# Block C's gates and output products by feature tile and spread over its steps, x in single k tiles, the last output bank in two halves

## The chip, the core and the metric

The kernel runs on one core of one Trainium2 chip. The core has a matrix engine (TensorE, PE in the profile), a vector engine (VectorE, DVE), an activation engine (ScalarE, ACT), GpSimd (POOL) and SyncE (SP), which here issues every DMA. The metric is the device time of one launch in microseconds (us), the median of some runs. The matrix engine multiplies a stationary block of 128x128, loaded into it by a weight load, with a moving operand of up to 512 columns, and adds up in PSUM, whose banks hold 512 float32 in each partition. Every engine works through its own instructions in the order in which the program has them.

## The reference

Three blocks over 256 tokens of width 1024: a retention layer (A), a latent attention layer (B), and a hybrid layer (C) of a recurrent branch, a sparse attention branch and a feed-forward network. A and B end in a layer norm. The change is mostly in C:

```
h = rms_norm(x, norm1_w);  u = h @ w_in          # split: rnn_x, rnn_gate, q, k, v, iq, ik, iw, g
xc = causal_depthwise_conv(rnn_x, conv_w, conv_b)
y_rnn = rg_lru(xc, ...) * gelu(rnn_gate)         # gates r, i; linear recurrence over the tokens
y_attn = dsa_attention(q, k, v, iq, ik, iw)      # top-64 keys by index score, softmax, 16 heads
gates = sigmoid(g + gate_b)                      # two branches of 1024 features
merged = gates[0] * (y_rnn @ w_o_rnn) + gates[1] * (y_attn @ w_o_attn)
x = x + merged @ w_out
x = x + square(relu(rms_norm(x, norm2_w) @ w_ff_in)) @ w_ff_out
```

## The kernel before

**Products in three parts.** Float32 operands are split into a rounded high part (`split`, L241 to L243: a cast on ACT, L242) and the rest as a low part (a subtraction on DVE, L243). A product is then three matmuls (`mm3`, L293 to L296: high by high, high by low, low by high, recorded as L294, L295 and L296).

**Weights in pieces.** `plan` lists all weights in the order of their use, as pieces of up to 1024 columns. `take` hands out the next piece and calls `fetch` for those up to seven further on (`AHEAD`): a DMA into a raw tile (4 buffers, or a `t2` tile for the small ones of the opening), then the split into a `whl` tile (8 buffers, two of which C's recurrence takes over). So each piece of 1024 costs ACT and DVE one instruction each, whatever product it goes into.

**Two forms of product.** `tpart` and `tgemm` have tokens on the partitions: the activation of 128 tokens is stationary and a piece of 512 features moves. `ftile` has features on the partitions: 128 features of the weights are stationary and 256 tokens move; one unit is 8 k tiles x 3 = 24 matmuls into one accumulator. Accumulators come from the pool `acc` of four PSUM banks; transposes use two banks (`tr`), attention two (`att`).

**The opening.** x and the first two weights come by k tiles, in groups of 1, 1, 2, 2 and 2 (`OPENING`); `values_and_gates` multiplies each group as it comes.

**The end of B.** `proj` runs B's output product; `norm1` calls `normal` (layer norm: sums on DVE, squares on ACT), then C's own norm and its transposes, for each half of the tokens.

**Block C.** Index projections, keys and values, and queries are `tgemm`s; the queries are copied by ACT (L993) and transposed at once. DVE picks 64 keys per token by eight rounds of `max` and `match_replace` (L983, L984) and writes the mask `sel` (L985). Then the table `STEPS` orders the rest by hand: `x` convolution of one feature tile (`conv`: a unit, then three DVE steps, L1085), `g` gelu gate (`gelu`: a unit, its second product on DVE is L1113), `z` recurrence gates (`gates`: two small float32 products, L1094, read by ACT at L1096 and L1097), `a` attention (`attend`: scores and softmax of one pair of heads, and the values of the pair before, all at high priority), `r` recurrence, `G` a gate product of 512 features (bias row added by DVE, L1151, then tanh), `O` an output product of 512 features (`gated`: times the gate, both branches added, transposed for the last product, L1152 to L1173). The four G and four O stand at the table's end. Within what the table and the priorities leave open, a scheduler puts each engine's instructions in order when the kernel is built.

**The end.** The feed-forward's output product adds up in four banks (two halves of the tokens by two halves of the features). After the last group each bank is scaled, added to x (L1262) and stored (L1263).

## Time and profile before

| what | value |
|---|---|
| time, 3 runs | median 893.03 us (891.98 to 893.21) |
| the profiled execution | 892.43 us, of which the span of its instructions 890.6 us |
| PE busy | 875.2 us (98%), 5471 matmuls |
| weight loads (PEld) busy | 784.4 us (88%) |
| DVE busy, ACT busy | 620.8 us (70%), 504.3 us (57%) |
| DMA | 157.16 MB, mean 176 GB/s |
| granted clock of PE | 1.00 throughout (2.4 GHz) |

Matmuls overlap each other in the records: one lasts longer than the distance to the next one's start. What a stream of them costs is read from the starts. Idle time of PE is listed with the engine and line that ended it; idle time of DVE and ACT costs nothing by itself.

### The profile page before, as it was taken

Reading aid. Unit: us, or ns where it says so; the run is one execution under the profiler, and the core shown is the slowest. Engines: PE = TensorE matmul, PEld = TensorE weight load, DVE = VectorE, ACT = ScalarE, POOL = GpSimd, SP = SyncE. Lnnn points to the kernel's source line nnn. Section 1 sums busy time; section 2 is a strip of 40 time slices with the busy share of each in tenths; the row PEclk is TensorE's granted clock in tenths of the full one; section 3 lists DMA queues with packets and bytes.
Section 4 is the critical chain, followed back from the end, with each engine's and each line's share of the span. In section 5 each row is a group of like instructions: output and inputs, shape, how many; then the busy total and the mean of one; then the engine's idle time right before and its main releaser. Section 6 shows DMA issues by size and latency. Waiting matters only on the chain.

```text
span 890.6 us, 14371 instructions
## 1 busy us (share of the span) xinstructions
PE 875.2 (98%) x5471; PEld 784.4 (88%) x5471; DVE 620.8 (70%) x1155; ACT 504.3 (57%) x860; POOL 40.8 (5%) x45
## 2 busy tenths in 40 slices
PE   8999999999999999999999999999999999999998
PEld 6988898889999999998878798987788889999997
DVE  5886776758766777676677799778766756555551
ACT  5644445435766676665458678987643455444440
POOL 0000000100100000002111020000000100000000
PEclk9999999999999999999999999999999999999999
DMA  8955455744654453546537634243765556556531
GB/s 295 310 190 171 160 170 185 274 134 159 231 166 153 144 165 132 177 143 247 185 116 223 216 100 148 84 143 119 248 203 179 187 164 212 190 188 190 190 119 48
DMA packets 47446, 157.16 MB, mean 176 GB/s; under 512 B 5392, under 2 KB 6160, under 8 KB 47248
## 3 DMA queue, kind: packets, MB, share of 16 engines
q1 hardware_dynamic: 47376, 156.23, 52.6%
q8 instruction: 43, 0.70, 0.3%
q14 instruction: 27, 0.22, 0.1%
HBM read 155.16 MB, written 1.05 MB: 175 GB/s over the span
## 4 chain that ended last, share of the span: by engine, by line
PE 86%; DVE 7%; ACT 2%; issue 2%; DMA 1%; SPq 0%; POOL 0%; ACTq 0%; DVEq 0%
PE acc L294 23%; PE acc L296 23%; PE acc L295 23%; PE att L294 4%; PE att L296 4%; PE att L295 4%; PE tr L215 2%; DVE whl L243 2%; DMA raw<-wpk 1%; PE att L1050 1%; DVE t L1085 1%; DVE s L984 1%; DVE sm L983 0%; DVE buf L1123 0%; PE att L404 0%
## 5 line engine op out<-in xcount | busy, mean ns | idle before, releaser
L243 DVE TENSOR_TENSOR whl<-raw,whl 128x1024 fp32r<-128x1024 f32 (+2 forms) x285 | 335.8, 1187 | 152.0 <-ACT whl L242 149.6
L242 ACT CAST whl<-raw 128x1024 fp32r<-128x1024 f32 (+2 forms) x285 | 288.3, 1021 | 218.1 <-PE acc L296 121.4
L294 PE MATMUL acc<-whl,s 128*128 128x512 f32 (+3 forms) x592 | 219.8, 377 | 2.5 <-DVE t L1151 1.2
L296 PE MATMUL acc<-whl,s 128*128 128x512 f32 (+3 forms) x592 | 221.6, 375 | 0.0
L295 PE MATMUL acc<-whl,s 128*128 128x512 f32 (+3 forms) x592 | 220.7, 373 | 0.5 <-DVE whl L243 0.5
L294 PE MATMUL acc<-s,whl 128*128 128x256 f32 x600 | 170.5, 284 | 2.7 <-ACT t L1097 1.3
L296 PE MATMUL acc<-s,whl 128*128 128x256 f32 x600 | 169.1, 282 | 0.0
L295 PE MATMUL acc<-s,whl 128*128 128x256 f32 x600 | 168.9, 282 | 0.0
L294 PEld LDWEIGHTS acc<-whl,s 128*128 128x128 f32 x592 | 111.3, 188 | 22.4 <-ACT whl L242 2.4
L296 PEld LDWEIGHTS acc<-whl,s 128*128 128x128 f32 x592 | 111.4, 188 | 18.9
L295 PEld LDWEIGHTS acc<-whl,s 128*128 128x128 f32 x592 | 111.4, 188 | 18.8 <-DVE whl L243 1.0
L294 PEld LDWEIGHTS acc<-s,whl 128*128 128x128 f32 x600 | 113.5, 189 | 4.3 <-ACT t L1097 1.7
L295 PEld LDWEIGHTS acc<-s,whl 128*128 128x128 f32 x600 | 113.5, 189 | 0.4
L296 PEld LDWEIGHTS acc<-s,whl 128*128 128x128 f32 x600 | 113.5, 189 | 0.1
L296 PE MATMUL att<-s,whl 128*128 128x256 f32 x224 | 62.9, 281 | 0.0
L294 PE MATMUL att<-s,whl 128*128 128x256 f32 x224 | 62.9, 281 | 0.0
L295 PE MATMUL att<-s,whl 128*128 128x256 f32 x224 | 62.9, 281 | 0.0
L294 PE MATMUL acc<-whl,hh 128*128 128x512 f32 x128 | 49.9, 389 | 0.0
L295 PE MATMUL acc<-whl,hh 128*128 128x512 f32 x128 | 49.8, 389 | 0.0
L296 PE MATMUL acc<-whl,hh 128*128 128x512 f32 x128 | 49.4, 390 | 0.0
L296 PEld LDWEIGHTS att<-s,whl 128*128 128x128 f32 x224 | 42.9, 191 | 0.1
L295 PEld LDWEIGHTS att<-s,whl 128*128 128x128 f32 x224 | 42.1, 188 | 0.6
(252 smaller groups left out, 1078.8 us busy)
## 6 DMA issues: line engine op xcount, KB each, us to landing
raw<-wpk SPq DMA_DIRECT2D x249, 512.0 KB, 4.1
raw<-wpk SPq DMA_DIRECT2D x32, 384.0 KB, 3.2
row<-rows SPq DMA_DIRECT2D x18, 256.0 KB, 6.5
t<-wpk SPq DMA_DIRECT2D x7, 256.0 KB, 5.6
raw<-wpk SPq DMA_DIRECT2D x4, 328.0 KB, 3.4
xs<-xtok SPq DMA_DIRECT2D x1, 1024.0 KB, 6.8
wb<-wab SPq DMA_DIRECT2D x4, 256.0 KB, 5.8
out<-t SPq DMA_DIRECT2D x4, 256.0 KB, 2.0
```

Source lines behind the costliest of these rows:

```text
L215: flips.append(nc.tensor.transpose(dst, src, ident))
L242: (copy or A.copy)(h, src)
L243: V.tensor_sub(l, src, h.bitcast(F32))
L294: return [mm(ps, lhsT=ah, rhs=bh, start=st, stop=False), mm(ps, lhsT=ah, rhs=bl, start=False, stop=False), mm(ps, lhsT=al, rhs=bh, start=F ...
L295: mm(ps, lhsT=ah, rhs=bl, start=False, stop=False),
L296: mm(ps, lhsT=al, rhs=bh, start=False, stop=sp)]
L984: V.match_replace(out=score[:, c], in_to_replace=s[:, 0:8], in_values=score[:, c], imm_value=GONE)
L1050: mm(o[:, 0:256], lhsT=vC[:, 0, g, j], rhs=pts[j][:, 0:256], start=j == 0, stop=False)
L1085: V.scalar_tensor_tensor(xc[:, d:], px[:, :256 - d], cw[:, m, j:j + 1], xc[:, d:], op0=ALU.mult, op1=ALU.add)
```

## The change

- x, and the first two weights with it, come in eight single k tiles.
- The gate and output products become `ftile` units: 16 `G` steps (8 for each branch) and 16 `O` steps of 128 features. The gate's bias is now a column and goes into the tanh on ACT; the four bias rows and their DVE additions go. A gate lies in 256 columns of a tile kept until its `O` step. `gated` leaves the result with features on the partitions, which is how the next product wants it: the 16 transposes behind it go, and its split reads the tile instead of PSUM.
- `STEPS` spreads x, G, z, g and a evenly; G10 to G17 run around the recurrence, the O steps stand at the end.
- The transposes of the queries are put off by two `take`s.
- In `attend`, matmuls and transposes lose their high priority; softmax, the copies behind the transposes and the split keep it.
- In `normal` the low parts of the `ckv` pieces fetched so far are ordered behind the mean.
- In the last group the fourth bank is closed one group earlier, added to x as `rest`, and the last products go in two halves of 256 columns into `tr` banks, each stored by itself.

```
-OPENING = ((0, 1), (1, 1), (2, 2), (4, 2), (6, 2))
+OPENING = tuple((k, 1) for k in range(8))
-STEPS = ("w0 w1 b x0 x1 x2 x3 g0 z0 g1 x4 a z1 g2 x5 a z2 g3 x6 a z3 g4 x7 a z4 g5 a z5 g6 a z6 g7 a "
-         "G00 z7 r a G01 a G10 G11 O00 O01 O10 O11").split()
+STEPS = ("w0 w1 b x0 G00 G01 x1 z0 g0 a x2 G02 z1 g1 a x3 G03 z2 g2 a x4 G04 z3 g3 a x5 G05 z4 g4 a x6 G06 z5 g5 "
+         "a x7 G07 z6 g6 a G10 z7 g7 a G11 r G12 G13 a G14 G15 G16 G17 "
+         "O00 O01 O02 O03 O04 O05 O06 O07 O10 O11 O12 O13 O14 O15 O16 O17").split()
...
+        low = split(hl[:, :w], hl[:, 1024:1024 + w], raw[:, :w])
+        if name == "ckv":
+            kvsplits.append(low)
...
-        V.tensor_scalar(nm, s[:, 0:1], s[:, 1:2], -1.0 / 1024.0, op0=ALU.add, op1=ALU.mult)
+        mean = V.tensor_scalar(nm, s[:, 0:1], s[:, 1:2], -1.0 / 1024.0, op0=ALU.add, op1=ALU.mult)
+        for low in kvsplits:
+            order(low, mean)
...
+            defer(DEFER_Q, lambda c=c, t=t, q=q: turn_queries(c, t, q))
...
+        urgent(softmax, p, scs, pbs, s, mx, nb)
...
-            A.copy(pt[:, :384], pp[:, :384])
+            urgent(A.copy, pt[:, :384], pp[:, :384])
...
-        split(ya[0][:, p], ya[1][:, p], o[:, 0:256])
+        urgent(split, ya[0][:, p], ya[1][:, p], o[:, 0:256])
...
-        with tc.high_priority():
-            nxt = scores(p + 1) if p < 7 else None
-            if p >= 0:
-                values(p, pend["pbs"])
+        nxt = scores(p + 1) if p < 7 else None
+        if p >= 0:
+            values(p, pend["pbs"])
...
-    def gate_gemm(br, n):
-        gb = row(f"gb{br}{n}")[0]
-        gps = tgemm(f"cg{br}", 4, hT)
-        for t in range(2):
-            w = gts[br, n, t] = t2()
-            V.tensor_add(w, gps[t], gb)
-            A.activation(out=w, in_=w, func=AF.Tanh, scale=0.5)
+    def gate(br, m):
+        ps = acc()[:, 0:256]
+        ftile(ps, take(f"cg{br}"), 0, hT)
+        if (br, m // 2) not in gts:
+            gts[br, m // 2] = rowp.tile([P, 512], F32, tag="row", name="gate") if (br, m) == (0, 0) else t2()
+        w = gts[br, m // 2][:, (m % 2) * 256:(m % 2) * 256 + 256]
+        A.activation(out=w, in_=ps, func=AF.Tanh, scale=0.5, bias=hbg[:, 8 * br + m:8 * br + m + 1])
...
+    def gated(br, m):
+        ps = acc()[:, 0:256]
+        ftile(ps, take(("cor", "coa")[br]), 0, (yr, ya)[br])
+        w, w0 = (gts[i, m // 2][:, (m % 2) * 256:(m % 2) * 256 + 256] for i in (br, 0))
         V.scalar_tensor_tensor(w, w, 1.0, ps, op0=ALU.add, op1=ALU.mult)
...
-        V.tensor_add(w, w, gts[0, n, t])
-        transposed(w, 4 * n, 4, mT, t, scale=0.5)
+        V.tensor_add(w, w, w0)
+        h, l = mT[0][:, m], mT[1][:, m]
+        A.activation(out=h, in_=w, func=AF.Copy, scale=0.5)
+        V.scalar_tensor_tensor(l, w, 0.5, h.bitcast(F32), op0=ALU.mult, op1=ALU.subtract)
...
+                corner = t == n == 1
+                if corner and g == NFG - 1:
+                    continue
...
+                if g == NFG - 1:
+                    store(t, c, fps[t][n], xs[:, t, c])
...
+        rest = t2()
+        V.scalar_tensor_tensor(rest, fps[1][1], r3[:, 1:2], xs[:, 1, 512:1024], op0=ALU.mult, op1=ALU.add)
+        for i in range(2):
+            c = slice(512 + i * 256, 768 + i * 256)
+            ps = tr()[:, 0:256]
+            for m in ms:
+                mm3(ps, hh[:, 0, m, tk], hh[:, 1, m, tk], pcs[m].h[:, 0, c], pcs[m].l[:, 0, c],
+                    m == 0, m == ms[-1])
+            store(1, c, ps, rest[:, i * 256:i * 256 + 256])
```

Three places show how the engines' orders move. The first is VectorE at the layer norm of the second half of the tokens at B's end: L553 makes the sums, L555 the mean (L555 and L557 after), L848 (L854) scales by it, and `whl` are splits of weight pieces. Before:

```order
L553 SCALAR_TENSOR_TENSOR t2_4876,sm_4878<-xs_1503,acc_4670 128x512
L243 TENSOR_TENSOR whl_4765<-raw_4763,whl_4765 128x1024
L553 SCALAR_TENSOR_TENSOR t2_4877,sm_4878<-xs_1503,acc_4671 128x512
L243 TENSOR_TENSOR whl_4926<-raw_4924,whl_4926 128x1024
L555 TENSOR_SCALAR sm_4878<-sm_4878 128x1
L848 SCALAR_TENSOR_TENSOR t2_4885<-t2_4876,sm_4878,row_4529 128x512
L848 SCALAR_TENSOR_TENSOR t2_4886<-t2_4877,sm_4878,row_4532 128x512
```

The same place after:

```order
L555 SCALAR_TENSOR_TENSOR t2_4919,sm_4921<-xs_1545,acc_4713 128x512
L555 SCALAR_TENSOR_TENSOR t2_4920,sm_4921<-xs_1545,acc_4714 128x512
L243 TENSOR_TENSOR whl_4969<-raw_4967,whl_4969 128x1024
L557 TENSOR_SCALAR sm_4921<-sm_4921 128x1
L243 TENSOR_TENSOR whl_4808<-raw_4806,whl_4808 128x1024
L854 SCALAR_TENSOR_TENSOR t2_4928<-t2_4919,sm_4921,row_4572 128x512
L854 SCALAR_TENSOR_TENSOR t2_4929<-t2_4920,sm_4921,row_4575 128x512
```

One of two splits ahead of the mean now stands directly behind it, still ahead of the two scalings.

The second place is VectorE in C's steps, at the last rounds of the choice of keys: MAX and MATCH_REPLACE are that choice, `qks` the stacked queries, L1085 the convolution (L1098 after), L1111 and L1113 the two products of a gelu gate (L1124 and L1126 after), `whl` splits of weights. Before, down to the mask:

```order
L243 TENSOR_TENSOR whl_5693<-raw_5691,whl_5693 128x1024
L1111 SCALAR_TENSOR_TENSOR t2_5766<-t2_5766,acc_5736 128x256
L983 MAX sm_5308<-s2_4922 128x8
L984 MATCH_REPLACE s2_4922<-sm_5290,s2_4922 128x128
L243 TENSOR_TENSOR whl_5739<-raw_5737,whl_5739 128x1024
L1085 SCALAR_TENSOR_TENSOR t2_5801<-acc_5771,pcol_1504,t2_5801 128x255
L984 MATCH_REPLACE s2_4922<-sm_5308,s2_4922 128x256
L1113 SCALAR_TENSOR_TENSOR buf_5547<-t2_5766,acc_5736 128x256
L985 TENSOR_SCALAR tab_4551<-s2_4922 128x128
L1085 SCALAR_TENSOR_TENSOR t2_5801<-acc_5771,pcol_1504,t2_5801 128x254
L985 TENSOR_SCALAR tab_4551<-s2_4922 128x256
```

The same place after:

```order
L243 TENSOR_TENSOR whl_5694<-raw_5692,whl_5694 128x1024
L1098 SCALAR_TENSOR_TENSOR t2_5721<-acc_5691,pcol_1546,t2_5721 128x253
L1124 SCALAR_TENSOR_TENSOR t2_5767<-t2_5767,acc_5737 128x256
L395 TENSOR_TENSOR qks_4960<-tr_5620,qks_4960 64x512
L990 MATCH_REPLACE s2_4965<-sm_5351,s2_4965 128x256
L991 TENSOR_SCALAR tab_4594<-s2_4965 128x128
L243 TENSOR_TENSOR whl_5740<-raw_5738,whl_5740 128x1024
L1126 SCALAR_TENSOR_TENSOR buf_5575<-t2_5767,acc_5737 128x256
L991 TENSOR_SCALAR tab_4594<-s2_4965 128x256
```

By the mask VectorE stood in the fifth convolution and the second gelu gate (`acc_5771`, `acc_5736`); it now stands in the second convolution and the first gelu gate (`acc_5691`, `acc_5737`).

The third place is VectorE at the program's end, which is new (L1278 is the last step of a bank, L1267 is `rest`):

```order
L1278 SCALAR_TENSOR_TENSOR t2_9334<-acc_7917,tiny_83,xs_1545 128x512
L1278 SCALAR_TENSOR_TENSOR t2_9343<-acc_7918,tiny_83,xs_1545 128x512
L1278 SCALAR_TENSOR_TENSOR t2_9352<-acc_7919,tiny_83,xs_1545 128x512
L1267 SCALAR_TENSOR_TENSOR t2_9355<-acc_7920,tiny_83,xs_1545 128x512
L1278 SCALAR_TENSOR_TENSOR t2_9364<-tr_9357,tiny_83,t2_9355 128x256
L1278 SCALAR_TENSOR_TENSOR t2_9374<-tr_9367,tiny_83,t2_9355 128x256
```

`rest`, whose bank is closed first of all, stands behind the step of the third bank.

## Rows read from the trace of the kernel before

**Rows 1.** The page, busy time of each engine (share of the span) and instructions:
```profile
PE 875.2 (98%) x5471; PEld 784.4 (88%) x5471; DVE 620.8 (70%) x1155; ACT 504.3 (57%) x860; POOL 40.8 (5%) x45
```

**Rows 2.** Waits of PE: line, releaser, us in total, times, longest:
```profile
PE att L1050 <- ACT t L1046: 1.5, 1, 1.5
PE acc L294 <- ACT t L1097: 1.3, 1, 1.3
PE acc L294 <- DVE buf L1113: 1.2, 1, 1.2
...
PE acc L294 <- DVE t L1151: 1.2, 1, 1.2
PE tr L215 <- ACT t L993: 1.1, 1, 1.1
PE tr L215 <- DVE t L819: 1.0, 1, 1.0
...
PE tr L215 <- ACT t L1046: 0.4, 1, 0.4
```

**Rows 3.** Timeline of PE (start, us, instruction) in three steady stretches; weight loads:
```profile
402.10 0.28 PE L295 MATMUL acc<-s,whl 128*128 128x256 f32 x1
...
403.98 0.28 PE L296 MATMUL acc<-s,whl 128*128 128x256 f32 x1
659.82 0.39 PE L294 MATMUL acc<-whl,s 128*128 128x512 f32 x1
...
663.94 0.39 PE L294 MATMUL acc<-whl,s 128*128 128x512 f32 x1
677.67 1.03 PE L215 MATMUL tr<-ident,t 128*128 128x128 f32 x8
L294 PEld LDWEIGHTS acc<-s,whl 128*128 128x128 f32 x600 | 113.5, 189 | 4.3 <-ACT t L1097 1.7
```

**Rows 4.** Busy time in stretches: PE, PEld, DVE, ACT, POOL, clock, DMA:
```profile
500.00:560.00 60.00, 55.70 (x429) 52.37 (x428) 55.17 (x171) 44.02 (x89) 6.56 (x4) 1.00 0.40 132
560.00:600.00 40.00, 40.00 (x256) 36.26 (x255) 30.06 (x92) 34.53 (x87) 0.00 (x0) 1.00 0.37 124
```

**Rows 5.** Timeline of PE in the opening, with idle time and releaser:
```profile
9.32 0.72 PE L294 MATMUL acc<-whl,s 128*128 128x512 f32 x2 [0.56 <-ACT whl L242]
12.97 0.50 PE L295 MATMUL acc<-whl,s 128*128 128x512 f32 x1 [0.54 <-DVE whl L243]
```

**Rows 6.** Timeline at B's last layer norm:
```profile
457.08 1.22 DVE L243 TENSOR_TENSOR whl<-raw,whl 128x1024 fp32r<-128x1024 f32 x1
458.21 0.21 DVE L555 TENSOR_SCALAR sm<-sm 128x1 f32<-128x1 f32 x1
458.46 1.42 DVE L848 SCALAR_TENSOR_TENSOR t<-t,sm,row 128x512 f32<-128x512 f32 x2
460.16 0.21 DVE L562 TENSOR_SCALAR sm<-sm 128x1 f32<-128x1 f32 x1 [0.28 <-ACT t L558]
```

**Rows 7.** Timeline at the start of C's steps:
```profile
510.77 0.65 PE L215 MATMUL tr<-ident,t 128*128 128x128 f32 x4 [1.06 <-ACT t L993]
510.96 0.61 DVE L983 MAX8 sm<-s 128x8 f32<-128x128 f32 x2
527.47 1.02 PE L1094 MATMUL acc<-t,wb 128*128 128x256 f32 x4
528.40 0.86 DVE L1085 SCALAR_TENSOR_TENSOR t<-acc,pcol,t 128x255 f32<-128x255 f32 x2
541.15 0.28 DVE L985 TENSOR_SCALAR tab<-s 128x256 f32<-128x256 f32 x1
```

**Rows 8.** The end: last matmul, last step, the stores; a step of 256 columns:
```profile
886.48 0.39 PE L296 MATMUL acc<-whl,hh 128*128 128x512 f32 x1
886.90 0.75 DVE L1262 SCALAR_TENSOR_TENSOR t<-acc,tiny,xs 128x512 f32<-128x512 f32 x1 [0.15 <-PE acc L296]
out<-t SPq DMA_DIRECT2D x4, 256.0 KB, 2.0
L1113 DVE SCALAR_TENSOR_TENSOR buf<-t,acc 128x256 f32<-128x256 f32 x8 | 3.3, 412 | 0.0
```

More of the change, by code (lines that the diff above doesn't have):

```diff
@@ L117, in plan @@
         elif op in "GO":
-            br, n = arg
-            for j in range(4):
-                if op == "G":
-                    o = og + br * 1024 + n * 512
-                    add(f"cg{br}", "c_in", 2 * j, 2, ar(o, o + 512))
-                else:
-                    add(("cor", "coa")[br], ("o_rnn", "o_att")[br], 2 * j, 2, ar(n * 512, n * 512 + 512))
+            br, m = arg
+            if op == "G":
+                o = og + br * 1024 + m * 128
+                add(f"cg{br}", "c_in", 0, 8, ar(o, o + 128))
+            else:
+                add(("cor", "coa")[br], ("o_rnn", "o_att")[br], 0, 8, ar(m * 128, m * 128 + 128))
     for k in range(8):
@@ L239, in body, with split @@
     wide_home = {}
-    def split(h, l, src, copy=None):
-        (copy or A.copy)(h, src)
-        V.tensor_sub(l, src, h.bitcast(F32))
+    def split(h, l, src):
+        A.copy(h, src)
+        return V.tensor_sub(l, src, h.bitcast(F32))
     def fetch():
@@ L988, in body, with turn_queries @@
     rq = tiny[:, 40:72].rearrange("p (t h) -> p t h", t=2)
+    def turn_queries(c, t, q):
+        p2 = tr()
+        for i in range(4):
+            transpose(p2[:, i * 128:i * 128 + 128], q[:, i * 128:i * 128 + 128])
+        p2 = p2.rearrange("p (k n) -> p k n", k=4)
+        if t == 0:
+            A.copy(q0[:, 4 * c:4 * c + 4], p2)
+        else:
+            stacked(p2, qs[c], 4)
     for c in range(2):
@@ L998, in body @@
             rsqrt(rq[:, t, c * 8:c * 8 + 8], s[:, 0:8], 8, 1.0, 64e-6)
-            p2 = tr()
-            for i in range(4):
-                transpose(p2[:, i * 128:i * 128 + 128], q[:, i * 128:i * 128 + 128])
-            p2 = p2.rearrange("p (k n) -> p k n", k=4)
-            if t == 0:
-                A.copy(q0[:, 4 * c:4 * c + 4], p2)
-            else:
-                stacked(p2, qs[c], 4)
+            defer(DEFER_Q, lambda c=c, t=t, q=q: turn_queries(c, t, q))
     yr = []
@@ L1022, in scores, with softmax @@
             half_product(scs[j][:, 128:384], parts(qs[blk], j, p % 4), kh[j][:, blk], kl[:, j, blk])
+        urgent(softmax, p, scs, pbs, s, mx, nb)
+        return pbs
+    def softmax(p, scs, pbs, s, mx, nb):
         for j in range(2):
@@ L1191, in body @@
         elif op == "G":
-            gate_gemm(*arg)
+            gate(*arg)
         else:
-            out_gemm(*arg)
+            gated(*arg)
     w2 = row("norm2")
@@ L1245, in ff_out, with store @@
                 c = slice(n * 512, n * 512 + 512)
+                corner = t == n == 1
+                if corner and g == NFG - 1:
+                    continue
                 for m in ms:
                     mm3(fps[t][n], hh[:, 0, m, tk], hh[:, 1, m, tk], pcs[m].h[:, 0, c], pcs[m].l[:, 0, c],
-                        g == 0 and m == 0, g == NFG - 1 and m == ms[-1])
+                        g == 0 and m == 0, g == NFG - 1 - corner and m == ms[-1])
+                if g == NFG - 1:
+                    store(t, c, fps[t][n], xs[:, t, c])
+        if g < NFG - 1:
+            return
+        rest = t2()
[7 more added lines that the diff above has]
+            store(1, c, ps, rest[:, i * 256:i * 256 + 256])
+    def store(t, c, ps, x):
+        o = t2()[:, :c.stop - c.start]
+        V.scalar_tensor_tensor(o, ps, r3[:, t:t + 1], x, op0=ALU.mult, op1=ALU.add)
+        dma(out[t * 128:t * 128 + 128, c], o)
     ff_in(0)
@@ L1257, in body @@
         ff_out(g)
-    for t in range(2):
-        for n in range(2):
-            c = slice(n * 512, n * 512 + 512)
-            o = t2()
-            V.scalar_tensor_tensor(o, fps[t][n], r3[:, t:t + 1], xs[:, t, c], op0=ALU.mult, op1=ALU.add)
-            dma(out[t * 128:t * 128 + 128, c], o)
 def constants():
@@ L1316, in pack @@
             "idxn": g["idx_k_norm_w_2"][0], "qkn": np.concatenate([g["q_norm_w_2"][0], g["k_norm_w_2"][0]])}
-    for br in range(2):
-        for n in range(2):
-            rowv[f"gb{br}{n}"] = g["gate_b_2"][0, br, n * 512:n * 512 + 512]
     flatrow = np.concatenate([rowv[n] for n, _ in ROWS])
```

22 lines of the change are left out of this document (6 added, 16 removed).

## The prediction

> **What bounds the kernel now.** I read the busy times first [rows 1]. PE is busy for 875.2 of the 890.6 us of the span (98%); DVE and ACT stand at 70% and 57%. So a change can only take PE's work away, or the 15 us in which PE stands still. The second view is the list of PE's waits [rows 2]: besides many of a few tenths there are seven single ones of 0.4 to 1.5 us, and all seven lie where this change moves something. The third is the spacing of the matmuls [rows 3], since their own lengths overlap: 256 columns take (403.98 - 402.10) / 16 = 0.118 us from start to start, 512 columns (663.94 - 659.82) / 18 = 0.229 us, a transpose about (1.03 - 0.28) / 7 = 0.11 us. The records last 0.28 and 0.39 us, 0.16 us more than the spacing. So a wait that lets the pipe run empty costs its listed time and 0.16 us on top. The fourth is a table of two stretches of C's steps [rows 4]: in 500 to 560 DVE is busy for 55.17 of 60 us, in 560 to 600 for 30.06 of 40. In the first it is the late engine, in the second it is not.
>
> **PE's own work.** Gates and output products in units of 24 matmuls of 256 columns instead of 12 of 512, and the end's 6 of 512 as 12 of 256: by the order of both kernels +780 matmuls of 256, -390 of 512 and -16 transposes. 780 x 0.118 - 390 x 0.229 - 16 x 0.11 = 92.0 - 89.3 - 1.8, about **+1.0 us**. There are 374 more weight loads, 189 ns each [rows 3]. I cost them at nothing, since the stretch at 402 us has one load of 189 ns for each matmul of 256 columns and yet starts one every 0.118 us: loads run beside matmuls and beside one another. Without that cover the price is rival C.
>
> The Trainium skill ("TensorE: Matmul & The Clock Gate", Part 3, "What overlaps and what doesn't") speaks against the change: it lets a weight load overlap matmuls in flight only where the row groups differ, and all loads here use all rows. By that rule the sum would be the one of rival C. The trace disagrees: loads of 189 ns fit between starts 118 ns apart [rows 3].
>
> **The opening.** x comes in eight pieces instead of five. PE waits twice [rows 5]: 0.56 us for the second k tile's split on ACT, 0.54 us for that of the third on DVE. The first six transfers are the same in both kernels, so the first wait stays. The third k tile is now half as large a transfer and half as long a split: that wait goes, 0.54 + 0.16 = **-0.7 us** (bounds 0 and -1.4).
>
> **B's last norm.** PE waits 1.04 us, shown as 1.0 [rows 2], for C's norm (L819), at the end of a chain on DVE and ACT: sums, a split of a weight piece (458.21 - 457.08 = 1.13 us), mean, two scalings (1.42), and the step at 460.16 that waits for the squares on ACT [rows 6]. The order takes one of two splits from ahead of the mean. It puts it directly behind, still ahead of the scalings. So the mean and with it the squares come 1.13 us earlier, but the scalings do not; the step at 460.16 now follows DVE's own queue, and of its wait of 0.28 us with the step from engine to engine about 0.35 is gained: **-0.35 us** (bounds 0 and -1.2, the whole wait and the drained pipe).
>
> **Queries.** Each query is transposed at once, and the last waits 1.06 us for the copy [rows 7]. Put off by two takes, the transposes stand behind a whole unit of 24 matmuls (24 x 0.118 = 2.8 us), which covers the copy: 1.06 + 0.16 = **-1.2 us** (bounds -0.7 and -1.3).
>
> **The steps' waits.** The other five of [rows 2] end on L1046 (twice, the copy of the transposed probabilities), L1097, L1113 and L1151. L1151 and its bias rows no longer exist; in the other places units G or x now stand between producer and user. What goes is 1.5 + 1.3 + 1.2 + 1.2 + 0.4 = 5.6, with 5 x 0.16 for the pipe **-6.4 us**. What is late next has to be put against it.
>
> **New: gelu 1.** There are four accumulator banks; the fifth user behind gelu 0 (x2, G02, the two of z1 in between) is gelu 1, and it takes gelu 0's bank. So it waits until DVE has done gelu 0's second product (L1113, L1126 after). DVE is without a gap from the first MAX at 510.96 to the mask's end at 541.15 [rows 7]. By the two orders the stretch that ends with that product of gelu 0 lacks, of the work that before did up to the mask, one split (1.13 [rows 6]), eight convolution steps (0.86 / 2 = 0.43 each [rows 7]) and two gelu products (0.41 each [rows 8]): 5.4 by durations, which overlap a little, so I take 5.0. That product is then done at about 541.15 - 5.0 = 536.2. PE, 1.06 us earlier at the first query's wait, has from 510.77 - 1.06 = 509.7 on seven units (168 x 0.118 = 19.8), 16 transposes (1.8), two z of 4 small products (1.02 - 0.16 = 0.86 each [rows 7]) and one pair's scores (8 matmuls of up to 256 columns, 0.9): it stands at gelu 1 at 533.9. The difference is 2.3, and 1.9 with the 5.4: **+2.0 us** for one wait. Bounds: 0, if DVE's split runs ahead as it may, and 4, if it is the full unit late.
>
> **New: the recurrence and the last pairs.** The last pair's transposes need some 18.5 to 19 us of DVE's and ACT's work behind gelu 7, and PE's units up to them make about 19 us. That is a tie. The same two instructions (L1046 to L1050) cost 1.5 before [rows 2]; my value is **+0.5 us** (bounds 0 and 1.5).
>
> **The tail.** Before, the last matmul starts at 886.48, a step of 0.75 us follows, and a store of 256 KB lands after 2.0 us [rows 8]. After, the last step has 256 columns (0.41 by L1113 [rows 8]), but it stands in DVE's queue behind the third bank's step and `rest`, 0.75 each. The third bank closes 12 x 0.118 = 1.4 us before the last matmul; 0.75 + 0.75 + 2 x 0.41 = 2.3 us from there is 0.9 behind the last matmul, just where the step before ended (0.15 + 0.75). So DVE brings nothing. The store is half as large. If its time went by its bytes it would gain 1.0 of the 2.0 us, if it is all fixed nothing; no row shows a store of 128 KB, and I take a tenth, nearer to fixed, since the other half's transfer goes out just ahead of it: **-0.2 us** (bounds +0.2, where DVE's steps come out longer, and -1.0).
>
> **The sum.** -0.7 - 0.35 - 1.2 - 6.4 + 1.0 + 2.0 + 0.5 - 0.2 = -5.35 us. The profiled execution took 892.43 us (its span 890.6), so it would be 887.1; the median is 893.03, and with the same difference it becomes **887.7 us** (0.994). A measurement of this kernel tells about 0.2% (1.8 us) from no change: faster is below 891.2, slower above 894.8.
>
> **Rivals.** (A) *No new wait.* DVE and ACT run ahead, since the copies and softmax keep their priority and the bias additions are gone. For it: 30.06 of 40 us busy in the second stretch [rows 4]. Against: DVE has no gap up to the mask [rows 7]. Without the 2.0 and 0.5: -7.85, that is 885.2 us. Chance 0.18.
> (B) *The waits come back elsewhere.* DVE's rounds of keys have as much work as before (55.17 of 60 us [rows 4]) and PE reaches them earlier, so banks come free late not once but at several gelu and convolution units, until the new waits are as large as the old: 6.4 in place of 2.5. Then -1.45, 891.6 us, no difference that can be told. Against: the order leaves convolutions for later that DVE did before the mask. Chance 0.12.
> (C) *Slower: the added weight loads show.* Where a unit's loads aren't hidden, 374 x 189 ns = 70.7 us come on top: 958 us. It decides from 7.1 / 374 = 19 ns for each added load on (no difference from 10 ns: 3.6 / 374). Against it stands the spacing at 402.10 [rows 3], in exactly that form of unit; for it only that the gates' stationary blocks come from pieces of another layout, and PEld is busy for 88% of the span already [rows 1]. Chance 0.05.
> (D) *Parts that do nothing.* The opening's wait only moves, the norm's chain ends with its scalings as before, the store costs the same: +1.25 on the forecast, 889.0 us. Chance 0.05.
>
> **How the numbers follow.** The forecast has 0.60, with a range of its own of 886.0 to 889.5 (the wait at gelu 1 between 0.5 and 3.5 and the tie between 0 and 1.5). The range of 8 in 10 is 884.0 to 891.6: from A with the opening at its better bound to B. C and half of B lie outside, and a little of the ends of A. Faster by over 0.2%: 0.60 + 0.18 + 0.05 and a little of B, 0.85; within: most of B, 0.10; slower: C, 0.05.
>
> **What would show it.** In the profile of the changed kernel PE's busy time rises by about 1 us, and 256 columns stay at 0.118 us from start to start in the G and O units; over 0.13 means C. The list of PE's waits has no L1151, no L993, and the one for L1126 at gelu 1 of 1 to 3 us near 534 to 536; several of over 1 us on DVE mean B, none means A. The wait at 12.97 is gone and the one at 9.32 still there. L819's wait is about 0.7. The last store lands as late behind the last matmul as before, or 0.3 us earlier. Wrong would be the prediction above all if DVE's order at the mask ran otherwise in time than I laid it out from the durations before.

## The result and the profile after

The changed kernel takes 886.95 us (median of six runs, 886.35 to 887.40) against 892.05 us before (six runs). The ratio is 0.994 with a 95% interval of 0.9928 to 0.9953, that is -5.1 us, between -4.2 and -6.4. The forecast was 887.7 us, -5.35. Of the profiled executions 892.43 us became 887.0; the spans are 890.6 and 885.2, both at a granted clock of 1.00 (2.4 GHz).

The sum came out, and several of its terms did not. The page of the changed kernel, busy time and instructions, to be held against [rows 1]:

```profile
PE 873.5 (99%) x5845; PEld 801.4 (91%) x5845; DVE 619.5 (70%) x1171; ACT 508.0 (57%) x881; POOL 39.1 (4%) x45
```

PE's waits in the changed kernel (line, releaser, us in total, times, longest), to be held against [rows 2]:

```profile
PE acc L296 <- DVE t2r L243: 2.3, 1, 2.3
PE acc L296 <- ACT tr L1012: 1.5, 1, 1.5
...
PE acc L296 <- DVE buf L1126: 0.8, 1, 0.8
PE tr L214 <- DVE t L825: 0.6, 1, 0.6
```

All five waits of the steps are gone, the copies of the probabilities (L1046) among them. The norm's wait (L825, L819 before) is down from 1.04 to 0.6. The queries' wait is still there, at another place and longer (L1012: 1.5 instead of L993: 1.1). The wait at gelu 1 (L1126) has come, with 0.8 instead of 2.0 us. And at the top stands one that the forecast does not have: 2.3 us for a split near 29 us. Timeline of ACT, DVE and PE there:

```profile
23.62 1.06 ACT L242 CAST whl<-raw 128x1024 fp32r<-128x1024 f32 x1 [0.18 <-DMA raw<-wpk]
26.88 1.05 ACT L242 CAST whl<-raw 128x1024 fp32r<-128x1024 f32 x1 [2.20 <-PE acc L298]
27.84 0.58 ACT L242 CAST t2r<-acc 128x512 fp32r<-128x512 f32 x1
...
27.96 1.22 DVE L243 TENSOR_TENSOR whl<-raw,whl 128x1024 fp32r<-128x1024 f32 x1 [2.02 <-ACT whl L242]
...
29.11 0.68 DVE L243 TENSOR_TENSOR t2r<-acc,t2r 128x512 fp32r<-128x512 f32 x1
...
29.84 0.39 PE L296 MATMUL acc<-s,whl 128*128 128x256 f32 x1 [2.29 <-DVE t2r L243]
```

Read it from the bottom. PE needs a bank of `acc`; the bank is free when DVE has split the values out of it (29.11); DVE needs ACT's copy (27.84), and ACT's copy stands in ACT's queue behind the copy of a large weight piece, for which ACT had stood idle for 2.2 us.

Where the time went can be read from three landmarks. Timeline of PE, the last product of the index scores and the last matmul, in the kernel before (the second is the first of [rows 8]) and in the changed one:

```profile
509.44 0.28 PE L404 MATMUL att<-ix 128*128 128x256 f32 x1
```

```profile
509.83 0.28 PE L406 MATMUL att<-ix 128*128 128x256 f32 x1
...
881.00 0.28 PE L298 MATMUL tr<-whl,hh 128*128 128x256 f32 x1
```

Up to the index scores the changed kernel loses 0.4 us (the opening loses 0.8, the norm gives 0.4 back). The 0.8 is one profile against one: the first matmul behind the opening starts anywhere from 28.1 to 29.4 us in the profiles of kernels with the old opening, and from 28.6 to 29.9 with the new one. From the last product of the index scores to the last matmul the changed kernel takes 371.17 us instead of 886.48 - 509.44 = 377.04: -5.9. From the last matmul's start to the end of the span it takes 4.2 us instead of 4.1.

### The profile page after: what moved, and what is told of

It reads as the page before. It is cut to its first block, busy times and chain, and to the rows that moved or that the text cites. A ratio compares the mean times of both kernels' runs of the same rounds, so it can differ in the third digit from the quotient of the medians.

```text
span 885.2 us, 15181 instructions
## 1 busy us (share of the span) xinstructions
PE 873.5 (99%) x5845; PEld 801.4 (91%) x5845; DVE 619.5 (70%) x1171; ACT 508.0 (57%) x881; POOL 39.1 (4%) x45
## 3 DMA queue, kind: packets, MB, share of 16 engines
HBM read 154.12 MB, written 1.05 MB: 175 GB/s over the span
## 4 chain that ended last, share of the span: by engine, by line
PE 94%; DVE 3%; ACT 2%; issue 1%; POOL 0%; DVEq 0%; ACTq 0%
PE acc L296 25%; PE acc L298 25%; PE acc L297 25%; PE att L296 4%; PE att L297 4%; PE att L298 4%; PE tr L214 3%; DVE whl L243 1%; PE att L1063 1%; PE acc L1107 1%; PE att L405 0%; PE att L406 0%; PE acc L452 0%; PE att L758 0%; PE att L730 0%
## 5 line engine op out<-in xcount | busy, mean ns | idle before, releaser
L243 DVE TENSOR_TENSOR whl<-raw,whl 128x1024 fp32r<-128x1024 f32 (+1 forms) x279 | 328.0, 1186 | 138.1 <-ACT whl L242 136.8
L242 ACT CAST whl<-raw 128x1024 fp32r<-128x1024 f32 (+1 forms) x279 | 282.1, 1020 | 215.3 <-PE acc L298 108.7
L296 PE MATMUL acc<-s,whl 128*128 128x256 f32 x856 | 243.6, 285 | 4.6 <-DVE t2r L243 2.3
L298 PE MATMUL acc<-s,whl 128*128 128x256 f32 x856 | 241.6, 282 | 0.0
L297 PE MATMUL acc<-s,whl 128*128 128x256 f32 x856 | 241.4, 282 | 0.0
L298 PE MATMUL acc<-whl,s 128*128 128x512 f32 (+3 forms) x464 | 171.0, 369 | 0.0
L297 PE MATMUL acc<-whl,s 128*128 128x512 f32 (+3 forms) x464 | 170.5, 368 | 0.0
L296 PE MATMUL acc<-whl,s 128*128 128x512 f32 (+3 forms) x464 | 169.7, 372 | 0.5 <-ACT s L242 0.5
L296 PEld LDWEIGHTS acc<-s,whl 128*128 128x128 f32 x856 | 161.7, 189 | 6.3 <-DVE t2r L243 2.7
L297 PEld LDWEIGHTS acc<-s,whl 128*128 128x128 f32 x856 | 162.3, 190 | 0.5
L298 PEld LDWEIGHTS acc<-s,whl 128*128 128x128 f32 x856 | 161.8, 189 | 0.2
L296 PEld LDWEIGHTS acc<-whl,s 128*128 128x128 f32 x464 | 87.5, 189 | 14.8 <-ACT s L242 1.3
L298 PEld LDWEIGHTS acc<-whl,s 128*128 128x128 f32 x464 | 87.4, 188 | 13.7
L297 PEld LDWEIGHTS acc<-whl,s 128*128 128x128 f32 x464 | 87.3, 189 | 12.7
L296 PE MATMUL acc<-whl,hh 128*128 128x512 f32 x126 | 49.1, 390 | 0.0
L297 PE MATMUL acc<-whl,hh 128*128 128x512 f32 x126 | 49.0, 389 | 0.0
L298 PE MATMUL acc<-whl,hh 128*128 128x512 f32 x126 | 48.8, 390 | 0.0
```

The source lines that it names most:

```text
L242: A.copy(h, src)
L243: return V.tensor_sub(l, src, h.bitcast(F32))
L296: return [mm(ps, lhsT=ah, rhs=bh, start=st, stop=False), mm(ps, lhsT=ah, rhs=bl, start=False, stop=False), mm(ps, lhsT=al, rhs=bh, start=F ...
L297: mm(ps, lhsT=ah, rhs=bl, start=False, stop=False),
L298: mm(ps, lhsT=al, rhs=bh, start=False, stop=sp)]
```

## The experiments

Ratios are to the kernel before, run beside each; the changed kernel's is 0.994. The span is that of the one profiled execution.

| kernel | ratio | 95% interval | span |
|---|---|---|---|
| e1_open | 1.0002 | 0.9992 to 1.0011 | 893.2 |
| e3_defer | 1.0004 | 0.9994 to 1.0013 | 891.3 |
| e12_prio | 0.9956 | 0.994 to 0.9973 | 886.8 |
| e4_steps | 0.9976 | 0.9964 to 0.9987 | 886.7 |
| e11_attend | 0.9941 | 0.9926 to 0.9956 | 885.4 |
| e2_last2 | 0.9928 | 0.9913 to 0.9943 | 885.3 |
| e8_valsplit | 0.9907 | 0.9891 to 0.9922 | 884.2 |
| e5_query | 0.9976 | 0.9964 to 0.9987 | 890.9 |
| e7_late | 0.9942 | 0.9927 to 0.9957 | 887.1 |
| e6_rest | 0.9931 | 0.9916 to 0.9946 | 883.7 |
| e9_best | 0.9892 | 0.9878 to 0.9907 | 882.1 |
| e10_gelu | 0.9889 | 0.9875 to 0.9904 | 881.8 |

The granted clock of PE is not 1.00 in all of these runs. In the profiles of e1_open, e7_late, e8_valsplit and e5_query it stands at 0.5 (1.2 GHz) for one stretch or two; the last section has the rows. Spans are therefore compared by stages below, and a difference of under 1 us between two kernels of the table is not read from times.

### The opening

**e1_open** is the kernel before with one line of the change:

```diff
-OPENING = ((0, 1), (1, 1), (2, 2), (4, 2), (6, 2))
+OPENING = tuple((k, 1) for k in range(8))
```

> The kernel before, with x and the first two weights in eight single k tiles and nothing else changed. Theory 1 (the opening costs): the waits of 0.56 and 0.54 us go, and a new one of about 2.3 us stands at the first unit of 256 columns near 28 us, as in the profile of the changed kernel; -0.56 - 0.54 - 2 x 0.16 + 2.3 + 0.16 is +1.0 us, a time ratio of about 1.001. Theory 2 (the prediction): one wait goes and nothing comes, -0.7 us; the new wait then belongs to some other part of the change.

Measured: +0.2 us (-0.7 to +1.0). Its list of waits has neither of the two of [rows 5] and a new one on top:

```profile
PE acc L294 <- DVE t2r L243: 2.0, 1, 2.0
```

So the 2.3 us belong to the opening, and they take back what the two old waits gave. The time alone decides nothing: the forecast's -0.7 lies at one edge of the interval and the +1.0 of theory 1 at the other. The new wait in the list speaks for theory 1. Of the two old waits the first is no firm gain: it is missing also from the lists of e3_defer and e12_prio, which have the old opening. The span of 893.2 holds, besides the wait, a stretch at a granted clock of 0.5 right behind it (29.7 to 33.1 us).

**e8_valsplit** changes only the order of two kinds of copies on ACT, in the changed kernel (piece 28 is the fifth large weight piece):

```diff
+        casts.append(A.copy(h, src))
...
+        piececast[i] = casts[-1]
...
                     for t in range(2):
                         split(*d["v"][t], vps[t])
+                        if h == 0:
+                            order(piececast[28], casts[-1])
```

> The changed kernel; only ACT's order is changed at 27 us: the rounding copies of the two value banks (first half of the split of the values) stand ahead of the copy of the fifth large weight piece, whose transfer lands at 26.85. Theory 1 (ACT waits in its queue for a late transfer, and the split that frees the bank stands behind it): the wait of 2.3 us goes, to 0 to 0.3; -2.2 to -2.4 us, a profiled span of about 883. Theory 2 (the banks are closed too late, three matmuls apart, for any split to be in time): most of the 2.3 us stays.

Measured: 0.9907, about 2.9 us less than the changed kernel's 0.994 (expected 2.2 to 2.4; the intervals of the two ratios reach 1.1 and 1.4 us to either side). The wait is not in its list any more, and the first matmul behind the opening starts at 27.4 us instead of 29.8. Theory 1 stands: the banks close early enough, and what cost the time was an instruction that waits for a transfer, ahead of one that had all it needed. The transfer is late because of the pieces: eight groups of half-size weight pieces go through `t2` tiles, so the first four large pieces take all four raw tiles at once, and the fifth cannot be issued before the first one's split on DVE ends. SyncE issues four of them from 13.97 us on, and the next at 22.15:

```profile
13.97 2.15 SPq L254 DMA_DIRECT2D raw<-wpk  x4
...
22.15 7.39 SPq L254 DMA_DIRECT2D raw<-wpk  x5
```

The piece issued at 22.15 is the one that ACT copies at 26.88. The releaser in the row at 26.88 is given as PE; by the program that copy waits for its transfer as well as for PE's use of the old piece (whose last matmul was done by about 25), and the transfer is the only one of the two that can end there.

**e2_last2** takes the last two k tiles of x together, in the changed kernel:

```diff
-OPENING = tuple((k, 1) for k in range(8))
+OPENING = tuple((k, 1) for k in range(6)) + ((6, 2),)
```

> The changed kernel; the last two k tiles of the opening come together (seven pieces of x instead of eight). Their weights then go through raw tiles, so the raw tiles come free earlier and the fifth large piece is fetched earlier. Theory 1 (late transfer ahead of the split in ACT's queue): the wait of 2.3 us goes and neither of the first two comes back: -2.3 us or a little more, span about 883. Theory 2 (the stream of transfers of the opening is the limit, whatever the pieces): the wait moves to another place with 1 to 2 us.

Measured: 0.9928, no difference from the changed kernel that can be told. Timeline of ACT:

```profile
25.16 1.05 ACT L242 CAST whl<-raw 128x1024 fp32r<-128x1024 f32 x1 [2.45 <-DMA raw<-wpk]
26.43 1.05 ACT L242 CAST whl<-raw 128x1024 fp32r<-128x1024 f32 x1 [0.22 <-DMA raw<-wpk]
27.39 0.57 ACT L242 CAST t2r<-acc 128x512 fp32r<-128x512 f32 x1
```

The transfer comes 1.7 us earlier and is named as the releaser now, but the order has a second large piece ahead of the value's copy, and the wait is 1.8 us. Of what I expected here only half held: the earlier transfer alone does not help where the queue's order stays. In the kernels with the changed kernel's opening the wait differs from profile to profile (0.4 in e4_steps, 1.0 in e6_rest, 1.9 in e7_late, 2.3 in the changed kernel), as one expects of a wait for a transfer.

### The queries and the stretch behind them

**e3_defer** is the kernel before with the transposes put off:

```diff
+            defer(2, lambda c=c, t=t, q=q: turn_queries(c, t, q))
```

> The kernel before; only the transposes of the queries are put off by two takes. Theory 1 (the wait only moves, since the unit that comes instead needs the bank that the query's square on ACT frees, behind eight activations of the index scores): a wait of about 1.5 us at the first convolution unit in place of 1.06 at the transposes, +0.3 to +0.5 us. Theory 2 (the prediction): the wait goes, -1.2 us.

Measured: +0.4 us (-0.5 to +1.2). The wait moved, as in theory 1: 1.1 us on L993 became 1.5 on the bank (L1005 in this kernel). By the landmarks used above it costs nothing in the end: from the last product of the index scores to the last matmul the profile takes 377.1 us, as before (377.0). Timeline of ACT in the changed kernel, which has the same order there:

```profile
507.54 0.95 ACT L975 ACTIVATE t<-att 128x384 f32<-128x384 f32 x2 [1.59 <-PE att L406]
508.85 0.95 ACT L975 ACTIVATE t<-att 128x384 f32<-128x384 f32 x2 [0.35 <-PE att L406]
510.15 0.49 ACT L975 ACTIVATE t<-att 128x384 f32<-128x384 f32 x1 [0.36 <-PE att L406]
510.54 0.58 ACT L1010 COPY t<-acc 128x512 f32<-128x512 f32 x1
511.00 0.61 ACT L1012 ACTIVATE tr<-acc 128x512 f32<-128x512 f32 x1
```

The four banks hold the four query accumulators. The first unit of the steps is their fifth user; it needs the first bank, which ACT reads twice (copy, square), and both stand behind the index scores' activations (L975), although ACT idles in between.

**e5_query** moves the code of the queries' product ahead of the loop over the index scores, in the changed kernel:

```diff
+    rq = tiny[:, 40:72].rearrange("p (t h) -> p t h", t=2)
+    def turn_queries(c, t, q):
...
+    for c in range(2):
+        ps = tgemm("cq", 4, hT)
...
     prio = tc.high_priority()
     prio.__enter__()
     for g in range(4):
```

> The changed kernel with the code of the queries' product moved ahead of that of the index scores, so that ACT copies and squares the queries of the first half before the eight activations of the index scores and not behind them; PE's products are the same. Theory 1 (the wait of 1.5 us at the first convolution unit is ACT's order, and it can be had back): it goes, and the wait at gelu 1 stays or grows by up to 1 us as PE comes there earlier: -0.7 to -1.7 us. Theory 2 (DVE bounds this stretch, whatever PE does): what is gained at the first unit is lost at gelu 1 or at the next units, 0 +- 0.5.

Measured: 0.9976, 3.2 us slower than the changed kernel by the ratios, worse than either theory. The wait of 1.5 us is gone, that on L1126 too, and one much larger has come, at the first pair of attention (timeline of PE in the first fence, of DVE in the second):

```profile
542.76 0.79 PE L1031 MATMUL att<-tab,s 128*128 128x128 f32 x2 [4.75 <-DVE sm L1039]
```

```profile
521.93 0.29 DVE L1014 MAX8 sm<-s 128x8 f32<-128x128 f32 x1
...
541.52 0.42 DVE L1016 TENSOR_SCALAR tab<-s 128x128 f32<-128x128 f32 x2
541.85 0.29 DVE L1039 CUSTOM_DVE_ANT_0 t<-att,tab 128x128 f32<-128x128 f32 x1
```

With the index scores behind the queries the rounds of keys begin at 521.9 instead of 511.4, and the mask, from which the softmax starts, is done at 541.9 instead of 536.9. Theory 2 was right about who bounds this stretch and too mild about the price. The price is not the wait alone. The profile is 5.7 us longer than the changed kernel's: the new wait less the two that went makes about 2.2 (4.9 - 1.7 - 0.95, each with the drained pipe); about 1.8 come from a granted clock of 0.5 at and behind that wait (540.0 to 546.8 us); and 1.6 from the same in the opening (31.4 to 34.8), which the edit doesn't touch. All ten runs have a mean granted clock of 0.994 to 0.998, all six of the changed kernel 1.0, so the 3.2 us can't be put down to the order of the code without that. The edit moved the index scores as well as ACT's copies, so it doesn't show what the copies alone would bring; that wasn't tried.

**e7_late** gives PE one more unit ahead of gelu 1, in the changed kernel:

```diff
...
-x2 G02 z1 g1 a x3 G03 z2 g2
+x2 G02 z1 G03 g1 a x3 z2 g2
...
```

> The changed kernel with step G03 moved from behind the third pair of steps to the place ahead of gelu 1, so that PE has one more unit (24 matmuls, 2.8 us) before it needs the bank that gelu 0's second product on DVE frees. Theory 1 (gelu 1 waits for DVE, as the prediction has it): the wait of 0.8 us goes, -0.8 to -1.0 us. Theory 2 (DVE is late at each of the next units too): the wait moves on to the next unit, 0 +- 0.3.

Measured: 0.9942, no difference, and the same wait of 0.8 us on L1126 in the list. Now the unit that follows z1, G03, waits. The banks go round by order of use: whoever is the fifth user behind gelu 0 gets its bank. I had the mechanism right and drew the wrong test from it. To shift the wait, work has to come between gelu 0 and the fifth user, not between that user and gelu 1, or DVE has to be done earlier. Of the two only the second was run (e10_gelu).

### What made the steps faster

**e4_steps** is the changed kernel with the old order of the table:

```diff
+STEPS = ("w0 w1 b x0 x1 x2 x3 g0 z0 g1 x4 a z1 g2 x5 a z2 g3 x6 a z3 g4 x7 a z4 g5 a z5 g6 a z6 g7 a "
+         "G00 G01 G02 G03 z7 r a G04 G05 G06 G07 a G10 ... G17 O00 ... O17").split()
```

> The changed kernel with the table of steps in the order of before: each G or O of 512 features becomes its four steps of 128 at the same place, none is spread between x, z, g and a. Theory 1 (the gain comes from the interleaving, which puts units between producer and user; the form by feature tile only removes the bias addition): the waits on L1110, L1126 and on the copy of the probabilities come back, about 1.3 + 1.2 + 1.5 + 0.4 us with their drained pipes and the small ones beside them, +5 to +6 us on the changed kernel, some 892. Theory 2 (the form itself gains, by the priorities and the missing transposes): +0 to +2 us.

Measured: 0.9976, 3.2 us slower than the changed kernel and 2.1 faster than before. Half of its eight runs have a mean granted clock of 0.997 or 0.998; its profile has 1.00, and there the steps, by the same landmarks, take 3.0 us longer than in the changed kernel (374.20 against 371.17). Timeline of PE:

```profile
508.27 0.28 PE L406 MATMUL att<-ix 128*128 128x256 f32 x1
...
882.47 0.28 PE L298 MATMUL tr<-whl,hh 128*128 128x256 f32 x1
```

So the table brings its part, about half of what theory 1 says; the rest came from elsewhere.

**e12_prio** is the kernel before with the priorities of attention alone:

```diff
-        with tc.high_priority():
-            nxt = scores(p + 1) if p < 7 else None
-            if p >= 0:
-                values(p, pend["pbs"])
+        nxt = scores(p + 1) if p < 7 else None
+        if p >= 0:
+            values(p, pend["pbs"])
...
+        urgent(softmax, p, scs, pbs, s, mx, nb)
...
+            urgent(A.copy, pt[:, :384], pp[:, :384])
...
+        urgent(split, ya[0][:, p], ya[1][:, p], o[:, 0:256])
```

> The kernel before with the priorities of attention alone as in the changed one: matmuls and transposes lose theirs; softmax, the copies and the split keep it. Theory 1 (table and form make the gain): the waits on L1097, L1113 and L1151 stay, those on L1046 (1.5 and 0.4 us) shrink or move: 0 to -1.5 us. Theory 2 (the priority makes most of it): -2.5 to -4 us.

Measured: 0.9956, -3.9 us (-2.4 to -5.4). Theory 2: with the old table and the old form, moving priority off PE's part of attention is worth about half of the whole change or more, three quarters by the medians. By the landmarks the steps take 373.48 us, 3.6 of the 5.9 gained there:

```profile
509.21 0.28 PE L404 MATMUL att<-ix 128*128 128x256 f32 x1
...
882.69 0.39 PE L296 MATMUL acc<-whl,hh 128*128 128x512 f32 x1
```

Its list of waits:

```profile
PE acc L294 <- ACT t L1100: 1.6, 1, 1.6
...
PE tr L215 <- ACT t L993: 1.1, 1, 1.1
PE tr L215 <- DVE t L819: 1.0, 1, 1.0
...
PE att L1053 <- ACT t L210: 0.5, 1, 0.5
PE acc L294 <- DVE buf L1116: 0.5, 1, 0.5
```

L1100, L1116 and L1053 are L1097, L1113 and L1050 of [rows 2]. The wait for the bias addition of a gate (L1151) is gone although that addition is still there; the copies' 1.5 and 0.4 are down to 0.5, L1113's 1.2 to 0.5. Only L1097 has not become smaller.

**e11_attend** is the counterpart: the changed kernel with these priorities as before.

```diff
+        with tc.high_priority():
+            nxt = scores(p + 1) if p < 7 else None
+            if p >= 0:
+                values(p, pend["pbs"])
```

> The changed kernel with attention's matmuls and transposes at high priority again, as before; the rest of the change stays. Theory 1 (the gain of the steps comes from the table and the form; the priority of PE's part is a detail): 0 to +1 us on the changed kernel. Theory 2 (at high priority PE takes up values and scores before their copies are done, and waits for them): the waits on the copied probabilities come back at several pairs, +2 to +4 us.

Measured: 0.9941, the same as the changed kernel. Two waits are larger (L1126 with 1.7, the copies with 0.9 us); only that of the opening is smaller. By the landmarks the steps take 371.57 us:

```profile
509.57 0.28 PE L406 MATMUL att<-ix 128*128 128x256 f32 x1
...
881.15 0.28 PE L298 MATMUL tr<-whl,hh 128*128 128x256 f32 x1
```

So table and form without the priorities give 5.5 of the 5.9 us, and the priorities alone give 3.6: what the two bring overlaps and is not to be added. They are no equal substitutes. With the table in place the priorities bring 0.4 us more; with the priorities in place (e4_steps) the table still brings 3.0. Three more kernels have this stretch as the changed kernel has it and 1.00 of the clock in it (e2_last2, e6_rest, e9_best): 371.3 to 371.5 us. So a difference of 3 us stands clear of noise. That each works by giving PE a unit of 24 matmuls to do while ACT and DVE finish a pair is argued, not shown.

### The tail, and a faster version

**e6_rest** writes `rest` at the head of the last group, in the changed kernel:

```diff
+        if g == NFG - 1:
+            rest = t2()
+            V.scalar_tensor_tensor(rest, fps[1][1], r3[:, 1:2], xs[:, 1, 512:1024], op0=ALU.mult, op1=ALU.add)
         for t in range(2):
...
-        rest = t2()
-        V.scalar_tensor_tensor(rest, fps[1][1], r3[:, 1:2], xs[:, 1, 512:1024], op0=ALU.mult, op1=ALU.add)
```

> The changed kernel; the step `rest` is written ahead of the last group's products, so that DVE makes it before the steps of the first three banks and not behind the third. Theory 1 (the tail is held by DVE's queue: three steps behind the last bank's closing): DVE's last step ends about 0.7 us earlier, -0.6 to -0.8 us. Theory 2 (the last store's transfer and what precedes it on its queue are the end): -0.2 us or less.

Measured: 0.9931, too close to 0.994 for the times to tell; the trace does tell. Timeline of DVE at the end of the changed kernel, and of e6_rest (whose last matmul starts at 880.09 and whose span ends at 883.7):

```profile
880.13 0.75 DVE L1278 SCALAR_TENSOR_TENSOR t<-acc,tiny,xs 128x512 f32<-128x512 f32 x1 [0.15 <-PE acc L298]
880.80 0.74 DVE L1267 SCALAR_TENSOR_TENSOR t<-acc,tiny,xs 128x512 f32<-128x512 f32 x1
881.64 0.88 DVE L1278 SCALAR_TENSOR_TENSOR t<-tr,tiny,t 128x256 f32<-128x256 f32 x2
```

```profile
879.22 0.75 DVE L1279 SCALAR_TENSOR_TENSOR t<-acc,tiny,xs 128x512 f32<-128x512 f32 x1 [0.16 <-PE acc L298]
879.88 1.01 DVE L1279 SCALAR_TENSOR_TENSOR t<-tr,tiny,t 128x256 f32<-128x256 f32 x2
```

DVE's last step ends 1.52 us behind the last matmul's start in the changed kernel and 0.80 in this one; the span ends 4.2 and 3.6 us behind it. So 0.6 us of the end were DVE's queue, as in theory 1.

**e9_best** is e8_valsplit and e6_rest together:

> The changed kernel with two of the former edits together: ACT's value copies ahead of the late large piece at 27 us, and `rest` written ahead of the last group. Theory 1 (the two are independent losses of the changed kernel): -2.2 - 0.6 = -2.8 us on it, a ratio to the kernel before of about 0.991. Theory 2 (the opening's gain is eaten by later transfers): about -1 us.

Measured: 0.9892, some 9.6 us under the kernel before; its span is 3.1 us below the changed kernel's, near the 2.8 expected. So the two gains add up.

**e10_gelu** adds an order on DVE at gelu 0, on top of e9_best:

```diff
...
+        first = V.scalar_tensor_tensor(w, w, 1.0, pg, op0=ALU.add, op1=ALU.mult)
...
-        V.scalar_tensor_tensor(tile8("gl", m), w, 1.0, pg, op0=ALU.add, op1=ALU.mult)
+        last = V.scalar_tensor_tensor(tile8("gl", m), w, 1.0, pg, op0=ALU.add, op1=ALU.mult)
+        if m == 0:
+            order(lows[193], first)
+            order(lows[194], last)
...
```

> The kernel of e9_best, and in DVE's order gelu 0's second product ahead of the split of one weight piece (1.13 us) that stood directly before it, and ahead of the first softmax. Theory 1 (the fifth user of the banks waits for DVE's queue, not for its own data): DVE is done 1.1 us earlier, the wait of 0.8 us on that product goes, -0.8 to -1.0 us on e9_best. Theory 2 (the split put off, or the softmax, makes a later unit wait): 0 +- 0.3, with a new wait within the next 10 us.

Measured: 0.9889, 0.3 us below e9_best, which the times can't tell apart. The wait on gelu 0's product is gone from the list and none has come in its place. From the last product of the index scores to the last matmul e9_best takes 371.45 us and e10_gelu 370.60, that is -0.85, as in theory 1; 0.6 of it is lost before that stretch, where the two kernels are the same and only the profiles differ. Timeline of PE in e9_best, then in e10_gelu:

```profile
507.08 0.28 PE L409 MATMUL att<-ix 128*128 128x256 f32 x1
...
878.53 0.28 PE L301 MATMUL tr<-whl,hh 128*128 128x256 f32 x1
```

```profile
507.66 0.28 PE L411 MATMUL att<-ix 128*128 128x256 f32 x1
...
878.26 0.28 PE L303 MATMUL tr<-whl,hh 128*128 128x256 f32 x1
```

e9_best and e10_gelu are the fastest kernels here, about 1.1% under the kernel before.

## Why the forecast held, and where it did not

| term | forecast | by trace or run | verdict |
|---|---|---|---|
| PE's own work | +1.0 | 0.118 us from start to start; about -0.6 left over in the steps | price right, sum not borne out |
| opening | -0.7 | +0.8 (one trace), +0.2 (e1_open) | wrong, a wait not seen |
| B's norm | -0.35 | -0.4 | right |
| queries | -1.2 | +0.5 (trace), +0.4 (e3_defer) | wrong, the wait moved |
| waits of the steps | -6.4 | all five gone | right in size, part of the reason missing |
| gelu 1 | +2.0 | +0.95 | right mechanism, PE came later |
| recurrence | +0.5 | 0 | too high |
| tail | -0.2 | +0.1 | within its bounds |

**PE's work and the loads.** In a stretch of gate and output units of the changed kernel stand 131 matmuls from the first of these to the second, all of 256 columns (timeline of PE):

```profile
643.71 0.28 PE L296 MATMUL acc<-s,whl 128*128 128x256 f32 x1
...
659.02 0.28 PE L297 MATMUL acc<-s,whl 128*128 128x256 f32 x1
```

15.31 / 130 is 0.118 us, the spacing of [rows 3], with a load of 189 ns for each: rival C is out. PE's busy time, though, did not rise by 1 us; it fell from 875.2 to 873.5. It is no measure of the work: each time the pipe runs empty the last record adds 0.16 us (0.28 against 0.118), so fewer interruptions make it smaller. That explains a part only: the traces have 22 gaps of PE before and 14 after, and 8 x 0.16 is 1.3 us, where 2.7 would be needed if the work had grown by 1.0. So the size of this term is not borne out.

**Opening.** The step that failed is "that wait goes". Both old waits went, the first too (which e3_defer and e12_prio show to come and go with the old opening); I looked at the pieces that PE waits for and not at the tiles that they pass through. Smaller pieces bypass the raw tiles, the four raw tiles fill up with large pieces at once, the fifth is late, and ACT's queue holds a split behind it (e8_valsplit). The bound given, 0 to -1.4, excluded a loss without a reason.

**Queries.** The step that failed is that a unit of 24 matmuls covers the copy. The unit itself is the fifth user of four banks and waits for the same engine. I counted the banks at gelu 1 and not here.

**gelu 1.** DVE was forecast to be done with gelu 0's second product at 536.2. Timeline of DVE and PE there:

```profile
535.03 1.22 DVE L243 TENSOR_TENSOR whl<-raw,whl 128x1024 fp32r<-128x1024 f32 x1
536.28 0.42 DVE L1126 SCALAR_TENSOR_TENSOR buf<-t,acc 128x256 f32<-128x256 f32 x1
...
536.75 0.39 PE L296 MATMUL acc<-s,whl 128*128 128x256 f32 x1 [0.79 <-DVE buf L1126]
```

It ends at 536.70, with the first MAX 0.4 us later than before: DVE's side was right to 0.1 us. PE was forecast at 533.9 and stood there at 536.0: the 1.06 us at the queries were not gained, 0.5 were lost on top, and the stretch began 0.4 later. So the terms were not independent: what PE loses ahead of a point at which DVE is the late engine is not lost twice. Queries and gelu 1 together were put at +0.8 and came to +1.5.

**The steps' waits.** All five went, -6.4, as forecast. From the last index score to the last matmul the trace shows -5.9; queries +0.5, gelu 1 +0.95, PE's work +1.0 and the five waits make -3.95. The missing 1.9 us can be placed in part. Between these landmarks PE is idle for 6.98 us in nine gaps before and for 2.63 in three after (-4.35), and the six gaps fewer, at 0.16 each for the drained pipe, give another 0.96. What is then left of the -5.9 is about -0.6, where the forecast has +1.0 for PE's own work; so most of the 1.9 stands against that term. Whether its price is too high or there were fewer stalls short enough to lie under the records is not shown. What was wrong in the reason: I gave the whole gain to the units between producer and user and did not price the change of priorities. e12_prio shows that the priorities alone bring 3.6 of the 5.9 us, e11_attend that table and form bring 5.5 without them.

**The last pairs and the tail.** The tie behind gelu 7 was put at +0.5, from two sums of about 19 us that no row shows; no wait came there. At the end "DVE brings nothing" failed: DVE's last step ends 1.52 us behind the last matmul's start, 1.17 before [rows 8], which cost 0.35, and the smaller store gave 0.3 back.

**A reading of the list.** The forecast counts seven single waits of 0.4 to 1.5 us; the full list behind [rows 2] also has 1.2 us behind L635, 0.4 behind L744 and the two of the opening. The opening has its own term; the other two are in both kernels with the same length, so the sum is not touched.

So the total came out within 0.3 us by luck: a wrong opening (1.5 us too good) and wrong queries (1.7 too good) were balanced by gelu 1 (1.05 too bad), the recurrence (0.5 too bad) and 1.9 us in the steps that no term has. What was right as a mechanism is that the steps' waits go, and that a wait on DVE comes at gelu 1. Of the rivals, A was nearest in the steps (one wait of 0.8 us came instead of two), B and C did not come, and of D the opening came, where the wait only moved.

## What to carry to other kernels

When a piece or a step gets smaller, count the users of each pool that it passes through, not only the wait that it is meant to shorten: the fifth user of four banks and the fifth piece of four raw tiles set both wrong terms here. In an engine's queue an instruction that waits for a transfer holds back those behind it that are ready; here it was worth more to look for one that stands ahead of a bank's release (e8_valsplit) than to bring the transfer earlier (e2_last2). Two edits that remove the same wait are not to be added: run each without the other before a gain is put down to one.

## What was not expected of the hardware

A store of 128 KB lands after 1.7 us where one of 256 KB takes 2.0 (DMA issues of the changed kernel); half the bytes save 0.3 us. An estimate from these two sizes: the larger part of such a store's time, about 1.4 us, does not go by its bytes.

```profile
out<-t SPq DMA_DIRECT2D x3, 256.0 KB, 2.0
out<-t SPq DMA_DIRECT2D x2, 128.0 KB, 1.7
```

The granted clock of PE fell in some profiles behind a wait and in others not. In e5_query it is 0.5 (1.2 GHz) in two stretches (columns as in [rows 4]; the third figure from the end is the clock):

```profile
31.40:34.80 3.40, 3.40 (x18) 3.40 (x18) 3.27 (x7) 2.85 (x5) 0.00 (x0) 0.50 0.85 275
540.00:546.80 6.80, 4.04 (x19) 4.04 (x20) 6.26 (x30) 4.93 (x15) 0.00 (x0) 0.50 0.22 77
```

Ahead of the first PE had waited for 2.2 us, up to 29.85; the second began within the wait of 4.75 us. In the second, matmuls of 256 columns start every 0.213 us instead of 0.118. In e1_open and e7_late the clock fell the same way behind the opening's wait (2.0 and 1.9 us), in e8_valsplit behind the queries' (1.5 us). In the changed kernel it did not fall, though its waits at these places are as long (2.3 and 1.5 us). So a wait of this length can cost about 1.6 us more than the list of waits says (e5_query's opening). Whether it does changes from run to run: the mean granted clock of e1_open is 0.998 in two of ten runs and 0.999 or 1.0 in the others.
